# Two heads of attention at a time, new estimates in the planner, two kinds of adds moved from GpSimd to VectorE, and a mixer table stored whole

## The chip, the cores and the metric

One core of one Trainium2 chip runs the kernel. The metric is the device time of one execution in microseconds (us). The engines are TensorE (PE; its weight loads are shown apart as PEld), VectorE (DVE), ScalarE (ACT), GpSimd (POOL) and SyncE (SP), which here issues every DMA. They run side by side and wait for one another by semaphores.

## What is computed

A decoder trunk of two layers on 512 positions of 1024 channels. Each layer has four parts: a half-step gated FFN, a token mixing of attention heads beside a state-space mixer (S5), a second half-step FFN, and a gated input embedding (ple).

```python
# per layer i:  h += 0.5*post(ffn1(h)); h += post(mix(h)); h += 0.5*post(ffn2(h)); h += post(ple(h))
def swiglu(x, w_gate, w_up, w_down):
    return (jax.nn.silu(x @ w_gate) * (x @ w_up)) @ w_down
...
q, k, v, u = jnp.split(rms_norm(h, mix_pre_g) @ w_in, [512, 1024, 1536], axis=-1)
q, k = partial_rotary(q, positions), partial_rotary(k, positions)   # 8 heads of 64
# three causal dilated windows (128,1),(512,4),(2048,16), merged by their softmax denominators
attn = dilated_mixture_attention(q, k, v)
# s5_mixer: 32 groups of 16 channels, 64 complex states each
lam_bar = jnp.exp(lam * dt); b_bar = ((lam_bar - 1.0) / lam)[..., None] * b_mat
_, states = lax.associative_scan(combine, (lam_bar, einsum(u, b_bar)), axis=1)
y = jnp.real(einsum(states, c_mat)) + d_skip * u
y = jax.nn.gelu(y); ssm = y * jax.nn.sigmoid(y @ w_glu + b_glu)
mixed = jnp.concatenate([rms_norm(attn, attn_norm_g), rms_norm(ssm, ssm_norm_g)], axis=-1)
h = h + rms_norm(mixed @ w_out, mix_post_g)
```

## The kernel before, in words

Activations lie transposed: 8 tiles of 128 channels by 512 positions. A product with a weight matrix is made in split precision: weight and activation are each parted into a high and a low float32r half, and `mm3` issues three matmuls (high by high, high by low, low by high) into one PSUM bank. The weights come as 392 units of up to 512 KB in the order of use; each is loaded by SP, its high half is written by ACT and its low half by DVE (128x1024, in the groups of the profile). A unit of 24 matmuls of 512 columns is then PE's work. The sections that close a part (`tail`, then `post`) go by two halves of 256 positions: PE works on the second half while DVE normalises the first and hands it to the next part.

No engine's order is written by hand. `Clock` keeps an estimated time for each engine and each word of memory; `Engine` adds an estimated cost for every instruction that is issued (`Engine.cost`, and the line with `ns =` in `mm`); side work runs in generators that yield the estimated time at which they want to go on, and `step` lets those run that are due before it issues the next three matmuls of the main stream. So every engine's order follows from these estimates: they are not executed, but whoever changes one changes the order.

The stretch with which the change has to do is the mixing (`mix`). The main stream is: u and the first q and k (6 units in halves), v (4 units), q and k of the second pair of heads, the GLU of the state-space branch, q and k of the other pairs, `w_out` in two parts. Beside it run three kinds of side work:

- **The mixer** (`mixer`, two lanes of two octets each; an octet is 8 groups). u is written to DRAM (`scratch_u`) and gathered by 8 DMAs (`gather_u`). For each octet SP loads tables (`tb`, `te`, `tc` from `scratch_t`) and the matrix T of the responses, which `ssm_prep` made in the FFN before and stored as 128x128 in `scratch_g`. T is block-triangular: POOL clears it once for each lane, and 8 DMAs of 64 down to 8 KB place shifted pieces of each response (lines 1517 and 1528 to 1532). PE's first product of an octet needs `tb` and the gathered u.
- **Attention** (`attention`, `head`). The three windows are one softmax with a mask of log counts. For each pair of heads t, and each block of 128 queries qi (3 down to 0), each of the two heads is a task of its own, 6 alive at most (`LIVE`). A task makes scores with two matmuls, one with all 128 rows and one with the head's own 64 rows (`q[rows, c], kl[rows, 0:W]`), then mask and minimum (DVE), exponent (ACT), reciprocal and scaling (DVE), qi+1 transposes (`flip`, line 568), a copy (ACT), and qi+1 products with v of 64 output columns (below: value products).
- **Sums of squares** (`sumsq`): ACT squares, POOL adds; and the rotary (`rotary`), whose last add is POOL's.

All DVE, ACT, POOL and SP instructions have line 353, all matmuls line 562, the transposes line 568. A plain float32 matmul leaves two records in the trace, a float32r matmul or a transpose one.

## Time and profile before

| | |
|---|---|
| median of 3 runs | 2147.78 us (2141.76 to 2147.9) |
| the profiled execution | 2144.88 us, its span 2143.1 us |
| PE busy | 2090.1 us, 98% |
| DVE, ACT, POOL busy | 1334.3, 798.4, 156.1 us |
| mixing, first product of the mixer to the output's tail | 443 to 614 us (layer 0), 1501 to 1672 us (layer 1) |

A row of the timeline merges instructions of one kind: its start, its time, and in brackets how long its engine was idle before it and what ended that. As matmuls are pipelined and their ends modelled, the spacing of a stream is read from one start to the next, or from a long row divided by its count.

### The profile page before, as it was taken

Reading aid. Unit: us, or ns where it says so; the run is one execution under the profiler, and the core shown is the slowest. Engines: PE = TensorE matmul, PEld = TensorE weight load, DVE = VectorE, ACT = ScalarE, POOL = GpSimd, SP = SyncE. Lnnn points to the kernel's source line nnn. Section 1 sums busy time; section 2 is a strip of 40 time slices with the busy share of each in tenths; the row PEclk is TensorE's granted clock in tenths of the full one; section 3 lists DMA queues with packets and bytes.
Section 4 is the critical chain, followed back from the end, with each engine's and each line's share of the span. In section 5 each row is a group of like instructions: output and inputs, shape, how many; then the busy total and the mean of one; then the engine's idle time right before and its main releaser. Section 6 shows DMA issues by size and latency. Waiting matters only on the chain.

```text
span 2143.1 us, 30766 instructions
## 1 busy us (share of the span) xinstructions
PE 2090.1 (98%) x11936; PEld 1780.0 (83%) x11936; DVE 1334.3 (62%) x2516; ACT 798.4 (37%) x1406; POOL 156.1 (7%) x167
## 2 busy tenths in 40 slices
PE   8999999989999999999999999998999999999997
PEld 7888888967789888889998888898777898888897
DVE  5887745776768975446674444467666864444474
ACT  4422333435554322223543222234356533222242
POOL 0000000101120000001200000011011200000022
PEclk9999999999999999999999999999999999999999
DMA  4424434471133534324324233246511333323131
GB/s 157 129 82 152 137 104 138 133 171 40 60 109 113 166 121 125 111 63 154 102 82 148 72 102 114 62 165 141 138 50 50 131 116 110 117 61 127 59 131 67
DMA packets 118145, 236.29 MB, mean 110 GB/s; under 512 B 27120, under 2 KB 58480, under 8 KB 118000
## 3 DMA queue, kind: packets, MB, share of 16 engines
q1 hardware_dynamic: 118000, 234.34, 35.3%
q8 instruction: 93, 1.52, 0.3%
q14 instruction: 52, 0.43, 0.1%
HBM read 208.60 MB, written 25.69 MB: 109 GB/s over the span
## 4 chain that ended last, share of the span: by engine, by line
PE 89%; DVE 6%; DMA 1%; issue 1%; ACT 1%; POOL 1%; SPq 0%; POOLq 0%; ACTq 0%; DVEq 0%
PE ps_all L562 88%; DVE sb_all L353 4%; DVE sr_all L353 2%; PE ps_all L568 1%; DMA sb_all<-scratch_t 1%; ACT sb_all L353 1%; POOL sb_all L353 1%; SPq L353 0%; ACT sr_all L353 0%; DVE z L353 0%; DMA sb_all<-weights 0%; DMA sb_all<-scratch_g 0%; DMA scratch_u<-sb_all 0%; ACT z L353 0%; POOLq L353 0%
## 5 line engine op out<-in xcount | busy, mean ns | idle before, releaser
L562 PE MATMUL ps_all<-sr_all 128*128 128x512 f32 (+2 forms) x7118 | 1447.2, 358 | 16.1 <-ACT sr_all L353 8.6
L562 PEld LDWEIGHTS ps_all<-sr_all 128*128 128x128 f32 (+1 forms) x7118 | 1185.1, 191 | 222.6 <-issue 19.2
L353 ACT ACTIVATE sr_all<-sb_all 128x512 fp32r<-128x512 f32 (+5 forms) x567 | 410.5, 742 | 562.7 <-DVE sb_all L353 398.9
L562 PE MATMUL ps_all<-sr_all,z 128*128 128x512 f32 (+1 forms) x2898 | 572.3, 348 | 0.9 <-DVE sr_all L353 0.9
L353 DVE TENSOR_TENSOR sr_all<-sb_all,sr_all 128x1024 fp32r<-128x1024 f32 (+5 forms) x455 | 417.8, 927 | 184.8 <-ACT sr_all L353 182.5
L562 PEld LDWEIGHTS ps_all<-sr_all,z 128*128 128x128 f32 x2898 | 469.8, 190 | 67.9 <-issue 1.8
L353 DVE TENSOR_TENSOR sb_all<-ps_all,sb_all 128x512 f32<-128x512 f32 (+1 forms) x396 | 244.4, 622 | 367.4 <-PE ps_all L562 361.7
L353 ACT ACTIVATE sb_all<-sb_all 128x256 f32<-128x256 f32 (+3 forms) x390 | 188.6, 490 | 483.2 <-DVE sb_all L353 481.1
L353 POOL TENSOR_TENSOR sb_all<-sb_all 128x256 f32<-128x256 f32 (+3 forms) x159 | 152.3, 960 | 1982.1 <-ACT sb_all L353 1739.1
L353 DVE TENSOR_TENSOR sb_all<-sb_all 128x256 f32<-128x256 f32 (+7 forms) x597 | 233.7, 407 | 22.6 <-DMA scratch_t<-sb_all 7.9
L353 ACT ACTIVATE sb_all<-ps_all 128x512 f32<-128x512 f32 (+5 forms) x228 | 102.9, 466 | 204.5 <-PE ps_all L562 166.8
L353 DVE SCALAR_TENSOR_TENSOR sb_all<-sb_all 128x512 f32<-128x512 f32 (+4 forms) x194 | 115.8, 599 | 65.0 <-ACT sb_all L353 63.3
L353 DVE TENSOR_TENSOR z<-sb_all,z 128x1024 fp32r<-128x1024 f32 (+2 forms) x112 | 120.2, 1075 | 55.3 <-ACT z L353 55.2
L562 PE MATMUL ps_all<-sb_all 128*64 128x128 f32 (+6 forms) x1412 | 127.4, 268 | 27.2 <-DMA sb_all<-scratch_t 12.6
L562 PEld LDWEIGHTS ps_all<-sb_all 128*64 128x64 f32 (+3 forms) x1412 | 108.1, 156 | 53.2 <-issue 27.1
L353 ACT ACTIVATE z<-sb_all 128x1024 fp32r<-128x1024 f32 (+2 forms) x112 | 103.5, 926 | 58.7 <-PE ps_all L562 39.2
L353 DVE TENSOR_SCALAR sb_all<-sb_all 128x32 f32<-128x32 f32 (+7 forms) x147 | 44.1, 306 | 37.3 <-POOL sb_all L353 20.7
L353 DVE SCALAR_TENSOR_TENSOR sb_all<-sb_all,ps_all 128x256 f32<-128x256 f32 x132 | 63.1, 480 | 4.3 <-PE ps_all L562 4.2
L353 DVE SCALAR_TENSOR_TENSOR sr_all<-sb_all,sr_all 128x256 fp32r<-128x256 f32 x96 | 51.8, 549 | 0.2 <-ACT sr_all L353 0.2
L353 DVE CUSTOM_DVE_ANT_0 sb_all<-ps_all,sb_all 128x512 f32<-128x512 f32 (+3 forms) x62 | 28.4, 485 | 34.5 <-PE ps_all L562 30.6
L568 PE MATMUL ps_all<-sb_all 128*128 128x128 f32 x218 | 33.9, 274 | 0.0
L568 PEld LDWEIGHTS ps_all<-sb_all 128*128 128x128 f32 x218 | 26.4, 140 | 7.3 <-issue 1.4
(38 smaller groups left out, 170.3 us busy)
## 6 DMA issues: line engine op xcount, KB each, us to landing
sb_all<-weights SPq DMA_DIRECT2D x263, 512.0 KB, 3.7
sb_all<-weights SPq DMA_DIRECT2D x96, 320.0 KB, 2.9
scratch_t<-sb_all SPq DMA_DIRECT2D x40, 256.0 KB, 3.2
scratch_h<-sb_all SPq DMA_DIRECT2D x80, 128.0 KB, 1.7
sb_all<-scratch_h SPq DMA_DIRECT2D x40, 256.0 KB, 5.8
sb_all<-scratch_t SPq DMA_DIRECT2D x16, 512.0 KB, 6.3
sb_all<-weights SPq DMA_DIRECT2D x32, 192.0 KB, 2.3
sb_all<-xt SPq DMA_DIRECT2D x16, 128.0 KB, 3.7
```

What stands on the lines that cost most here:

```text
L353: return f(*a, **k)
L562: self.nc.tensor.matmul(out, lhsT, rhs, start=start, stop=stop)
L568: self.nc.tensor.transpose(out, x, self.ident)
```

## The change

The planner's estimates are other numbers: latency behind PE 200 ns in place of 170; a float32r matmul at least 110 ns; 100 ns where a matmul's weights change between more and at most 64 rows or columns; a DMA at least 450 ns, and by the length of its runs, with 4000 ns to landing in place of 2000 where these are 512 bytes or less; more for DVE instructions with a per-partition scalar and for the shuffle. `sumsq` and `rotary` add on DVE. `ssm_prep` keeps each response behind 112 cleared columns and stores 8 shifted copies into `scratch_r`, 128x1024 for each octet, and `mixer` loads T from there with one DMA of 512 KB and clears nothing. Attention takes the two heads of a pair in one task (`block`, 3 alive): for qi 0 and 1 both share a PSUM bank and a copy; the second score matmul has all 128 rows, for which `parts` keeps a low half of k for each head in both halves of the partitions (6 slots of the float32r store in place of 5, and two ACT copies of 64x512 more for each pair of heads); and the value products of the two heads alternate.

```diff
-LIVE = 6
+LIVE = 3
-    LAT = 170.0
+    LAT = np.array([200.0, 170.0, 170.0, 170.0, 170.0])
+    SHAPE = 100.0
...
-            self.ck.take(self.name, self.cost(op, outs, ins, k), outs, ins, 2000.0 if op == "dma_start" else 0.0)
+            done = 0.0
+            if op == "dma_start":
+                done = 2000.0 if self.run(*outs, *ins) > 512 else 4000.0
+            self.ck.take(self.name, self.cost(op, outs, ins, k), outs, ins, done)
...
-            return n * outs[0].shape[0] * 4 / 330.0
+            b = n * outs[0].shape[0] * 4
+            return max(450.0, b / 330.0, b / self.run(*outs, *ins) * 2.4)
...
-            return 65 + 0.52 * n
-        return 70 + {"reciprocal": 8.3, "tensor_tensor_scan": 2.08}.get(op, 1.04) * n
+            return 65 + 0.52 * n + 60 * sum(n > words(x) == 1 for x in ins)
+        own = sum(n > words(x) == 1 for x in ins) * 60 + 165 * (op == "stream_shuffle")
+        return 70 + own + {"reciprocal": 8.3, "tensor_tensor_scan": 2.08}.get(op, 1.04) * n
...
-        ns = max(n, lhsT.shape[1]) / 0.6 / share + 4 if lhsT.dtype == F32 else n / 2.4 + 2.5
+        ns = max(n, lhsT.shape[1]) / 0.6 / share + 4 if lhsT.dtype == F32 else max(n / 2.4 + 13.3, 110.0)
+        shape = lhsT.shape[0] > 64, lhsT.shape[1] > 64
+        if shape != self.ck.shape:
+            self.ck.shape = shape
+            ns += self.ck.SHAPE
...
-            self.tt(acc, acc, v, ALU.add, eng=self.po)      # sumsq
+            self.tt(acc, acc, v, ALU.add)
-        self.tt(dst, dst, self.b(b), ALU.add, eng=self.po)  # rotary
+        self.tt(dst, dst, self.b(b), ALU.add)
...
-        gv = self.b(ws)[:, 4 * NW:4 * NW + P]
+        gz = self.b(ws)[:, 4 * NW:4 * NW + (2 * L - 1) * GC]
+        gv = gz[:, (L - 1) * GC:]
+        self.po.memset(gz[:, 0:(L - 1) * GC], 0.0)
...
-            self.sy.dma_start(self.scratch_g[i, o], gv)
...
-            yield self.ck.after(3000.0)
+            for j in range(L):
+                yield self.ck.after(1500.0)
+                self.sy.dma_start(
+                    self.scratch_r[i, o, j * GC:(j + 1) * GC].rearrange("h (g c) -> g h c", g=2 * Q),
+                    gz[:, j * GC:j * GC + P])
...
-        self.po.memset(T, 0.0)
...
-            src = self.scratch_g[i, o].rearrange("(g h) c -> h g c", h=GC)
-            for ti in range(L):
-                j = L - 1 - ti
-                self.sy.dma_start(Tv[j * GC:(j + 1) * GC, :, ti * GC:], src[:, :, 0:(L - ti) * GC])
+            self.sy.dma_start(T, self.scratch_r[i, o])
...
-    def head(self, M, t, hh, qi, bank):
+    def block(self, M, t, qi, bank):
...
-        self.mm(self.pb(bk, W), q[:, c], k[:, 0:W], True, False)
-        self.mm(self.pb(bk, W), q[rows, c], kl[rows, 0:W], False, True)
+        for (q, k, kl), s in zip(parts, sc):
+            self.mm(s, q[:, c], k[:, 0:W], True, False)
+            self.mm(s, q[:, c], kl[:, 0:W], False, True)
...
+        if one:
+            self.act(self.b(bufs[1], 2 * W), self.pb(bks[0], 2 * W))
...
-        for j in range(n):
-            self.mm(self.ps[rows, bank * SEQ + qi * P:bank * SEQ + (qi + 1) * P],
-                    self.b(v[j])[:, t * P + hh * HD:t * P + (hh + 1) * HD], self.b(pt)[:, j * P:(j + 1) * P],
-                    j == 0, j == n - 1)
+        for j in range(n):
+            for hh in range(2):
+                rows = slice(hh * HD, (hh + 1) * HD)
+                self.mm(self.ps[rows, bank * SEQ + qi * P:bank * SEQ + (qi + 1) * P],
+                        self.b(v[j])[:, t * P + hh * HD:t * P + (hh + 1) * HD], pt[hh][:, j * P:(j + 1) * P],
+                        j == 0, j == n - 1, 2)
...
-        got = yield from self.rs.tgets(1, 1, 1, 1, 1)
+        got = yield from self.rs.tgets(1, 1, 1, 1, 1, 1)
...
+        for _, _, l, own, other in heads:
+            self.act(l[other], l[own].bitcast(F32))
```

Every engine's order is new. In the rows below one row is a run of like instructions; PE's float32 matmul is one instruction here.

PE, layer 0, from the last 128x128 that spreads the norm (all of u waits for it) to the first products of the mixer (64x64), before:

```order
L562 MATMUL ps_all<-sb_all 128x1 x2
L562 MATMUL ps_all<-sb_all 128x128 x2
L562 MATMUL ps_all<-sr_all 128x256 x57
L562 MATMUL ps_all<-sr_all,z_75 128x256 x24
L562 MATMUL ps_all<-sr_all 128x256 x24
L562 MATMUL ps_all<-sr_all 128x512 x27
L562 MATMUL ps_all<-sb_all 64x64 x16
L562 MATMUL ps_all<-sr_all 128x512 x18
```

and after:

```order
L583 MATMUL ps_all<-sb_all 128x1 x2
L583 MATMUL ps_all<-sb_all 128x128 x2
L583 MATMUL ps_all<-sr_all,z_75 128x256 x6
L583 MATMUL ps_all<-sr_all 128x256 x96
L583 MATMUL ps_all<-sr_all 128x512 x57
L583 MATMUL ps_all<-sb_all 64x64 x16
L583 MATMUL ps_all<-sr_all 128x512 x18
L583 MATMUL ps_all<-sb_all 64x64 x16
```

The mixer's first product stands behind 57 matmuls of 512 columns and 102 of 256 in place of 27 and 105; in layer 1 behind 54 in place of 30. These are v's.

PE, layer 0, the end of the last pair's attention (128x384, x256 and x128 from `sr_all` alone are scores, 64x128 value products, rows of the other line transposes, the rest `w_out`), before:

```order
L562 MATMUL ps_all<-sr_all,z_4015 128x512 x3
L568 MATMUL ps_all<-sb_all 128x128 x4
L562 MATMUL ps_all<-sb_all 64x128
L562 MATMUL ps_all<-sr_all 128x256 x2
L568 MATMUL ps_all<-sb_all 128x128 x6
L562 MATMUL ps_all<-sr_all,z_4015 128x512 x3
L562 MATMUL ps_all<-sb_all 64x128 x4
L562 MATMUL ps_all<-sr_all 128x256 x2
L562 MATMUL ps_all<-sb_all 64x128 x4
L562 MATMUL ps_all<-sr_all,z_4015 128x512 x3
L562 MATMUL ps_all<-sb_all 64x128 x6
L562 MATMUL ps_all<-sr_all 128x128 x2
```

and after:

```order
L593 MATMUL ps_all<-sb_all 128x128 x8
L583 MATMUL ps_all<-sb_all 64x128 x2
L583 MATMUL ps_all<-sr_all,z_4023 128x512 x3
L593 MATMUL ps_all<-sb_all 128x128 x6
L583 MATMUL ps_all<-sr_all 128x256 x4
L583 MATMUL ps_all<-sr_all,z_4023 128x512 x3
L583 MATMUL ps_all<-sb_all 64x128 x14
L583 MATMUL ps_all<-sr_all,z_4023 128x512 x3
L583 MATMUL ps_all<-sr_all 128x128 x4
L583 MATMUL ps_all<-sr_all,z_4023 128x512 x9
L593 MATMUL ps_all<-sb_all 128x128 x4
L583 MATMUL ps_all<-sr_all,z_4023 128x512 x3
```

Two heads' scores and value products stand together where each head's stood apart. In the whole program the 160 value products, 224 transposes and 128 score matmuls are as many as before; the 64 score matmuls of 64 rows have 128.

SP, layer 0, from the gathering of u on, before:

```order
L353 DMA sb_all<-scratch_u 16x32x64 x8
L353 DMA sb_all<-scratch_t 128x1024
L353 DMA sb_all<-scratch_t 128x512
L353 DMA sb_all<-scratch_t 128x1024
L353 DMA sb_all<-scratch_g 16x8x128
L353 DMA sb_all<-scratch_g 16x8x112
L353 DMA sb_all<-scratch_g 16x8x96
L353 DMA sb_all<-scratch_g 16x8x80
L353 DMA sb_all<-scratch_g 16x8x64
L353 DMA sb_all<-scratch_g 16x8x48
L353 DMA sb_all<-scratch_g 16x8x32
L353 DMA sb_all<-scratch_g 16x8x16
```

and after:

```order
L358 DMA sb_all<-scratch_u 16x32x64 x8
L358 DMA sb_all<-scratch_t 128x1024
L358 DMA sb_all<-scratch_t 128x512
L358 DMA sb_all<-scratch_t 128x1024
L358 DMA sb_all<-scratch_r 128x1024
L358 DMA sb_all<-scratch_t 128x1024
L358 DMA z_3388<-scratch_t 128x512
L358 DMA sb_all<-scratch_t 128x1024
L358 DMA sb_all<-scratch_r 128x1024
L358 DMA sb_all<-weights 128x1024 x4
```

Eight loads of T have become one, and the second lane's tables follow four issues behind the first lane's in place of eleven. In the FFN before, 8 stores to `scratch_g` have become 64 to `scratch_r` (2 to 3 in a row between weights). On POOL 124 of 159 adds and powers are gone, 96 of them 128x256 and 28 128x512; DVE has them.

## Rows read from the trace of the kernel before

**Rows 1.** The page, busy us of an engine, share of the span, instructions.

```profile
PE 2090.1 (98%) x11936; PEld 1780.0 (83%) x11936; DVE 1334.3 (62%) x2516; ACT 798.4 (37%) x1406; POOL 156.1 (7%) x167
```

**Rows 2.** The page, shares of the chain that ended last.

```profile
PE 89%; DVE 6%; DMA 1%; issue 1%; ACT 1%; POOL 1%; SPq 0%; POOLq 0%; ACTq 0%; DVEq 0%
```

**Rows 3.** Busy time by stretch: us, PE, PEld, DVE, ACT, POOL busy (instructions), clock, DMA.

```profile
653.00:1011.00 358.00, 358.00 (x1831) 302.94 (x1830) 226.44 (x391) 114.63 (x173) 8.29 (x10) 1.00 0.39 124
1011.00:1021.00 10.00, 9.06 (x67) 8.25 (x65) 9.83 (x21) 4.41 (x11) 3.90 (x5) 1.00 0.01 2
443.20:613.80 170.60, 166.67 (x1136) 124.38 (x1136) 117.25 (x279) 85.75 (x180) 18.71 (x13) 0.97 0.29 83
1501.40:1671.60 170.20, 165.48 (x1132) 125.65 (x1132) 114.80 (x279) 85.33 (x180) 19.21 (x13) 0.96 0.28 78
613.80:652.60 38.80, 36.38 (x286) 35.72 (x286) 33.70 (x72) 18.36 (x44) 12.71 (x16) 0.96 0.39 140
```

**Rows 4.** PE in order of time, layer 0's attention: start, us, instructions.

```profile
465.22 1.09 PE L562 MATMUL ps_all<-sb_all 128*64 128x128 f32 x16
...
499.21 0.70 PE L562 MATMUL ps_all<-sr_all 128*128 128x256 f32 x2
499.84 0.87 PE L562 MATMUL ps_all<-z,sb_all 128*64 128x128 f32 x6
...
514.13 10.48 PE L562 MATMUL ps_all<-sr_all 128*128 128x512 f32 x45
...
580.52 1.09 PE L562 MATMUL ps_all<-sb_all 128*64 128x128 f32 x8
...
583.41 0.58 PE L562 MATMUL ps_all<-sr_all 128*128 128x128 f32 x2
583.92 0.65 PE L562 MATMUL ps_all<-sb_all 128*64 128x128 f32 x4
...
620.18 7.72 PE L562 MATMUL ps_all<-sr_all 128*128 128x256 f32 x63
```

**Rows 5.** PE in order of time, where it waits in either layer's mixing.

```profile
443.23 1.97 PE L562 MATMUL ps_all<-sb_all 128*64 128x64 f32 x32 [5.50 <-DMA sb_all<-scratch_t]
...
643.24 1.05 PE L562 MATMUL ps_all<-sb_all 128*128 128x1 f32 x8 [1.66 <-POOL sb_all L353]
...
1501.36 1.98 PE L562 MATMUL ps_all<-sb_all 128*64 128x64 f32 x32 [7.10 <-DMA sb_all<-scratch_t]
```

**Rows 6.** Groups by line and shape: busy us, mean ns, idle before.

```profile
L353 DVE TENSOR_TENSOR sb_all<-sb_all 128x256 f32<-128x256 f32 x273 | 120.0, 441 | 7.8 <-ACT sb_all L353 0.5
...
L353 POOL TENSOR_TENSOR sb_all<-sb_all 128x256 f32<-128x256 f32 x99 | 83.2, 843 | 1458.4 <-ACT sb_all L353 1450.0 <-DVE sb_all L353 3.4 <-issue 3.1
...
L353 POOL TENSOR_TENSOR sb_all<-sb_all 128x512 f32<-128x512 f32 x28 | 43.6, 1561 | 337.8 <-DVE sb_all L353 210.6 <-ACT sb_all L353 118.7 <-issue 5.4
L353 DVE TENSOR_TENSOR sb_all<-sb_all 128x512 f32<-128x512 f32 x65 | 43.1, 688 | 8.4 <-DMA scratch_t<-sb_all 5.7 <-DMA scratch_u<-sb_all 1.8
...
L353 ACT ACTIVATE sr_all<-sb_all 64x512 fp32r<-64x512 f32 x48 | 30.1, 627 | 16.2 <-POOL sb_all L353 15.6
```

**Rows 7.** SP's queue in order of time, layer 0: start, us, issues.

```profile
434.75 2.42 SPq L353 DMA_DIRECT2D sb_all<-scratch_t  x3
437.29 8.51 SPq L353 DMA_DIRECT2D sb_all<-scratch_g  x8
```

**Rows 8.** POOL and DVE in order of time, a stretch of squares' sums.

```profile
621.85 5.22 POOL L353 TENSOR_TENSOR sb_all<-sb_all 128x256 f32<-128x256 f32 x6 [4.42 <-ACT sb_all L353]
...
626.60 0.76 DVE L353 TENSOR_TENSOR sb_all<-sb_all 128x256 f32<-128x256 f32 x1
...
628.04 0.42 DVE L353 TENSOR_TENSOR sb_all<-sb_all 128x256 f32<-128x256 f32 x1
```

More of the change, by code (lines that the diff above doesn't have):

```diff
@@ L243, in peek @@
             m, s = self._span(ap)
-            t = max(t, (m[0][s] + np.where(m[1][s] != c, self.LAT, own)).max())
+            t = max(t, (m[0][s] + np.where(m[1][s] != c, self.LAT[m[1][s]], own)).max())
         for ap in outs:
@@ L1619, in rotary @@
         self.stt(self.b(b), self.b(b), scale, self.b(M["sin"]))
-        self.tt(dst, dst, self.b(b), ALU.add, eng=self.po)
+        self.tt(dst, dst, self.b(b), ALU.add)
         self.sl.put(b)
-    def head(self, M, t, hh, qi, bank):
+    def block(self, M, t, qi, bank):
         v = M["v"]
-        q, k, kl = (self.r(b) for b in M["parts"][t][hh])
+        parts = [[self.r(b) for b in x] for x in M["parts"][t]]
         n = qi + 1
         W = n * P
-        rows = slice(hh * HD, (hh + 1) * HD)
-        yield self.ck.ready(q, k, kl[rows])
-        while len(self.sl.free) < 2:
+        one = 2 * W <= SEQ
+        yield self.ck.ready(*[x for p in parts for x in p])
+        need = 2 if one else 4
+        while len(self.sl.free) < need:
@@ L1655, in head @@
-        self.sl.put(p)
-        yield self.ck.ready(self.b(pt, W))
-        for j in range(n):
-            self.mm(self.ps[rows, bank * SEQ + qi * P:bank * SEQ + (qi + 1) * P],
-                    self.b(v[j])[:, t * P + hh * HD:t * P + (hh + 1) * HD], self.b(pt)[:, j * P:(j + 1) * P],
-                    j == 0, j == n - 1)
-        self.sl.put(pt)
+        bufs = [self.sl.get() for _ in range(need)]
+        p = [self.b(bufs[0])[:, hh * W:(hh + 1) * W] if one else self.b(bufs[hh], W) for hh in range(2)]
@@ new lines, in block @@
+        pt = [self.b(bufs[1])[:, hh * W:(hh + 1) * W] if one else self.b(bufs[2 + hh], W) for hh in range(2)]
+        c = slice(qi * P, (qi + 1) * P)
+        bks = []
+        sc = []
+        for hh in range(2):
+            if not (one and hh):
+                bks.append((yield from self.tbank()))
+            sc.append(self.pb(bks[-1], W, W * hh if one else 0))
+        for (q, k, kl), s in zip(parts, sc):
+            self.mm(s, q[:, c], k[:, 0:W], True, False)
+            self.mm(s, q[:, c], kl[:, 0:W], False, True)
@@ new lines, in block @@
+        dens = []
+        for hh in range(2):
+            st = self.o_st + 2 * (self.nst % 32)
+            self.nst += 1
+            m, den = self.w(st, 1), self.w(st + 1, 1)
+            dens.append(den)
+            self.ve.tensor_tensor_reduce(
+                out=p[hh], in0=sc[hh], in1=self.w(self.o_const + C_MASK + SEQ - W, W), scale=-1.0,
+                scalar=3e38, op0=ALU.add, op1=ALU.min, accum_out=m)
+            self.act(p[hh], p[hh], AF.Exp, scale=-1.0, bias=m, accum_out=den)
@@ new lines, in block @@
+        self.free(*bks)
+        for hh in range(2):
+            yield self.ck.ready(p[hh])
+            self.ve.reciprocal(dens[hh], dens[hh])
+            self.ts(p[hh], p[hh], dens[hh])
+        yield self.ck.ready(*p)
+        bks = []
+        for hh in range(2):
+            if not (one and hh):
+                bks.append((yield from self.tbank()))
+            for j in range(n):
+                self.flip(self.pb(bks[-1], P, (W * hh if one else 0) + j * P), p[hh][:, j * P:(j + 1) * P])
+            if not one:
+                self.act(pt[hh], self.pb(bks[-1], W))
@@ L1673, in parts @@
             self.act(a[own], q[own])
-        yield max(self.ck.written(a[own]) for a, _, own, _ in heads)
-        for a, _, own, other in heads:
+        yield max(self.ck.written(a[own]) for a, _, _, own, _ in heads)
+        for a, _, _, own, other in heads:
             self.tt(a[other], q[own], a[own].bitcast(F32), ALU.subtract)
         yield self.ck.written(k)
-        for _, b, own, _ in heads:
+        for _, b, _, own, _ in heads:
             self.act(b[own], k[own])
-        yield max(self.ck.written(b[own]) for _, b, own, _ in heads)
@@ L1681, in parts @@
-        for _, b, own, other in heads:
-            self.tt(kl[own], k[own], b[own].bitcast(F32), ALU.subtract)
+        yield max(self.ck.written(b[own]) for _, b, _, own, _ in heads)
+        for _, b, l, own, other in heads:
+            self.tt(l[own], k[own], b[own].bitcast(F32), ALU.subtract)
             self.act(b[other], k[own])
+        yield max(self.ck.written(l[own]) for _, _, l, own, _ in heads)
+        for _, _, l, own, other in heads:
+            self.act(l[other], l[own].bitcast(F32))
@@ L1684, in parts @@
         self.sl.put(M["q"][t], M["k"][t])
         M["rs"][t] = got
-        M["parts"][t] = [(got[2 * hh], got[2 * hh + 1], got[4]) for hh in range(2)]
+        M["parts"][t] = [tuple(got[3 * hh:3 * hh + 3]) for hh in range(2)]
     def attention(self, i, M):
@@ L1697, in attention @@
             for qi in range(3, -1, -1):
-                for hh in range(2):
-                    while sum(not d[0] for d in live) >= LIVE:
-                        yield self.ck.after(100.0)
-                    d = self.ck.spawn(self.head(M, t, hh, qi, bank))
-                    live.append(d)
-                    mine.append(d)
-                    live = [d for d in live if not d[0]]
+                while sum(not d[0] for d in live) >= LIVE:
+                    yield self.ck.after(100.0)
+                d = self.ck.spawn(self.block(M, t, qi, bank))
+                live.append(d)
+                mine.append(d)
+                live = [d for d in live if not d[0]]
             ends.append(self.ck.spawn(self.attended(i, t, M, bank, mine)))
```

50 lines of the change are left out of this document (24 added, 26 removed).

## The prediction, as it was made

> **What bounds the kernel now.** The page's busy shares come first: PE 2090.1 of 2143.1 us [rows 1]; then the chain, 89% PE and 6% DVE [rows 2]. So PE's stream sets the time, and the question is what it holds besides useful columns, and where it stands still. Busy time by stretch says where [rows 3]: in an FFN (653 to 1011) PE has no gap at all, so nothing can be won there by another order. The mixing is different. From the mixer's first product to the tail of `w_out` it takes 170.6 us in layer 0 and 170.2 in layer 1, PE nearly full, DVE busy 117.25 and 114.80 (69 and 67%). Between parts DVE is the full one: 9.83 of 10 us from 1011 on, 33.70 of 38.80 at the end of layer 0's mixing. Last I read PE in order of time inside the mixing, for the price of single products, and its waits.
>
> **Scores.** A long run of 45 matmuls of 512 columns takes 0.233 us each, one of 63 with 256 columns 0.1225 [rows 4]; the line through both gives 0.067 for 128. A head's score pair of 256 columns should thus take 0.245 and takes 0.63 from its start to the next row's (499.21 to 499.84); one of 128 should take 0.13 and takes 0.51 (583.41 to 583.92). The excess is 0.385 and 0.38. The pair holds the one matmul with 64 rows, and the array goes over to it and back. After, all scores have 128 rows and the change of shape is gone. 64 pairs at 0.38: 24.3 us off PE's stream. If the excess were half a cost of small batches that stays, 12; more than 24.3 isn't to be seen.
>
> **Value products.** Four of one head take 1.09 us and two 0.65, so one takes 0.22; eight of the mixer's products of the very same shape (128 rows, 64 columns, 128 moving), whose halves of the columns alternate, take the same 1.09 [rows 4]. Alternating, a product costs half. 160 of them save 160 x 0.11 = 17.6; some stood by chance next to the other head's already, and I take 15. Bounds: 0, were they not to overlap, and 17.6 with up to 2 us more for the fewer groups.
>
> **The wait for the first table.** PE stands 5.50 us at 443.23 and 7.10 at 1501.36 until the table behind the gathered u has landed [rows 5]. The new order puts 30 and 24 matmuls of 512 columns (v) before that product, 30 x 0.233 = 7.0 and 24 x 0.233 = 5.6 us. The gather itself starts where it did, behind the same norm. So the first wait goes and 1.5 of the second stays: 11 us. These matmuls are missing later as filler, but PE still has q and k of the second pair (45 matmuls on end at 514 [rows 4]) when the lanes are done, so I charge nothing; were the filler missed, all 11 come back.
>
> **What DVE gets.** 96 adds of 128x256 at 0.441 and 28 of 128x512 at 0.688 (POOL's took 0.843 and 1.561) are 61.6 us of new DVE work [rows 6]. In the FFNs it lies beside PE, with DVE at 226.44 of 358. At the seams DVE is full, and there an add on it delays the next part's first operands. The two seams mixing to FFN are solid DVE work for 20 us: six adds of the second half, 6 x 0.44 = 2.6 each, 5.3 together. The others have PE work in stock (ple's up-projection, the first half's products of u). Against it, PE waited for POOL's slow last add, 1.66 us at 643.24 [rows 5] and so at some other seams, partly ended now. Net +2 (bounds -6.6, four such waits given back and the adds covered, and +21, the adds paid at eight seams).
>
> In the mixing the stretch loses 19.6 us of PE work (half of 24.3 + 15) and 7.0 or 5.6 that went ahead, 144.0 and 145.0 remain. DVE has there some 12 of the 128x512 adds more, 8.2: 125.5 and 123.0, which is 87 and 85%. That is much for a queue in order, on which weight splits, two mixer lanes and masks stand between one another; I charge 2 us a layer, 4 (bounds 0 and 25: the rival below). ACT's 16 copies of 64x512, 0.627 each [rows 6], are 10 us on an engine that is half idle (85.75 of 170.6); they delay each pair's first score by under 1 us, while other pairs run.
>
> **T and its stores.** SP needed 8.51 us for the eight loads of one octet [rows 7]; one load takes about 0.4. But PE's first wait is for what stands before T in the queue, and the next lane's table, 8 us earlier, meets a PE that has v to do: 0 (bounds -3 and +1, as 512 KB replace 288). The 56 further stores, 64 KB each, in FFNs: DMA is busy there at 0.39 [rows 3], and if they hold up a weight load it is by their issue of about 0.4 us; the units are loaded three ahead. 0 (up to +3).
>
> **One rule against the change.** [Rows 8]: while POOL works through six adds without a break to 627.07, a DVE add of 128x256 that starts at 626.60 takes 0.76 us, the next, alone, 0.42. The Trainium skill, SBUF — State Buffer, "SBUF: two separate sides", says that VectorE and GpSimd share one pair of ports under an exclusive lock and that an instruction on the one shuts the other out as a whole. By that rule the moved adds are cheaper than their durations: if each of the 124 had held up DVE by 0.34, DVE would get 42 of its 61.6 us back, and the seams' +2 would be about -1. The trace agrees where DVE has work just then; elsewhere it isn't shown, and the sum goes by the durations.
>
> **Sum.** -24.3 - 15 - 11 + 2 + 4 = -44.3 us. Against the profiled execution's 2144.9 that is 2100.6; the median of the runs lies 2.9 above it, within their spread, so I say 2101.
>
> **Rivals.** (1) *DVE limits the mixing.* Its 125.5 us need a share that no whole stretch of the mixing has yet had; for it speaks the 69%, against it the seams, where it runs at 98%. If 79% is its best, the stretches take 159 and 156: 1.5 us (v in front of the first product, where only 5.50 were idle) - 11.6 - 14.2 + 2 = -22.3, 2123. The Trainium skill, TensorEngine Tiling (Array Packing), "PSUM Bottleneck", warns of just this: tiling speeds up TensorE, not the evacuation of PSUM. (2) *DVE paces it as it stands*, its gaps being the latency of chains and not want of work: then its share stays 69 and 67%, the stretches take 183 and 182, 12.4 and 11.8 more than before, and with 1.5 + 2 the kernel takes 2173, slower. It decides from a share below some 74% (248.5 us of DVE in the 337 of both stretches that would leave the sum at nothing). Against it: PE idles only 3.9 and 4.7 us there [rows 3], so DVE's gaps are times when PE was the late one. (3) *Alternating value products don't overlap in attention*, because each pair waits for its own copies: 2116. The copies of both heads are done before the first product, which speaks against it. (4) *The waits shrink too*, as the estimates now know more of what PE waits for: the idle 3.9 and 4.7 go, and the 2 and 4 charged to DVE don't come, 14.6 less: 2086. (5) *The change doesn't do what it says* in the table load: worth 0 in any case.
>
> **Chances.** Forecast 0.58, own range 2092 to 2111; (4) 0.17; (1) 0.17; (3) 0.05; (2) 0.03. The range leaves out the slow rival and the ends of (1) and (4): 2083 to 2125. About 0.3%, 6.4 us, can be told from no change here. Faster: all but (2) and the outer part of (1), 0.94; within, 0.03; slower, 0.03.
>
> **What would show it.** No matmul with 64 rows by 128 columns is left, and two score pairs of 256 columns follow each other at about 0.12 a matmul; sixteen records of value products take about 1.09. At the mixer's first product the wait is gone in layer 0 and under 2.5 in layer 1. The stretch from there to the tail is 143 to 149 us long, DVE at 85% or more, and PE's idle time in it below 10 us. At the seam out of the mixing DVE's solid work is up to 2.6 us longer. It would be wrong if PE's waits for DVE in the mixing rose above 15 us a layer, if the wait for the table came back elsewhere (for T, or as idle time before the GLU), or if attention started so late that its last pair ended behind `w_out`'s first part.

## The result, and the profile after

The changed kernel takes 2160.35 us (median of 7 runs, 2154.46 to 2165.54) against 2147.78: ratio 1.0066, 95% interval 1.0051 to 1.0081. Forecast were 2101 us, 2083 to 2125. It is slower by 0.7%, and the profile shows that TensorE's work shrank all the same.

The page's busy times and its chain, to be held against [rows 1, 2], and the span with the mean granted clock, before (first row of the second block) and after:

```profile
PE 2062.0 (96%) x11936; PEld 1773.6 (82%) x11936; DVE 1357.6 (63%) x2640; ACT 803.2 (37%) x1406; POOL 27.5 (1%) x41
...
PE 76%; DVE 15%; ACT 4%; issue 3%; DMA 2%; SPq 1%; POOL 0%; ACTq 0%; DVEq 0%; POOLq 0%
```

```profile
core 0: 2143.1 us, clock 0.988
core 0: 2154.3 us, clock 0.979
```

PE is busy 28 us less, and idle 2154.3 - 2062.0 = 92.3 us where it was 53.0. DVE's part of the chain went from 6 to 15%. With two levels, 2.4 and 1.2 GHz, a mean clock of 0.979 means that 2 x 0.021 x 2154 = 90 us ran at the lower one; before, at 0.988, it was 51. An estimate from this: the 39 us more at half the clock cost at most 20 us of PE's busy time, so its products themselves became 28 to 48 us cheaper.

Where it went, by stage, from the first product of one part to that of the next (us of the profiled executions; two numbers are the two layers; the four columns on the right are runs told of below):

| stage | before | after | u_adds | late | u_T | late_T_slack |
|---|---|---|---|---|---|---|
| FFN 1 of layer 0, seventh projection to closing | 311.7 | 316.4 | 315.0 | 315.0 | 315.0 | 311.7 |
| into the mixing, up to v | 41.7, 40.4 | 45.2, 47.0 | 42.4, 42.4 | 39.6, 39.6 | 47.1, 45.2 | 39.6, 39.6 |
| v to `w_out`'s tail | 179.9, 181.9 | 167.9, 165.7 | 166.6, 166.2 | 167.3, 169.7 | 162.5, 166.1 | 161.5, 163.5 |
| out of the mixing | 27.5, 27.6 | 35.0, 33.1 | 27.5, 27.6 | 28.9, 30.7 | 35.6, 33.4 | 30.7, 27.2 |
| FFN 2, first six projections | 42.5, 42.5 | 47.0, 46.8 | 40.5, 40.5 | 47.4, 42.1 | 43.0, 43.4 | 39.5, 39.5 |
| FFN 2 of layer 0, the rest | 311.8 | 316.0 | 314.9 | 315.9 | 313.8 | 311.7 |

The mixings gained 28.2 us. The six stretches around them lost 31.9, the two FFNs beside which the next table is prepared 8.9; the other stages gained 1.4. That is the 11.2 us between the two profiled executions.

The mixing as the forecast had cut it, from the first mixer product on (columns as in [rows 3]):

```profile
452.20:609.60 157.40, 138.85 (x1105) 111.09 (x1104) 116.73 (x289) 87.71 (x178) 1.05 (x1) 0.95 0.27 95
1518.10:1673.30 155.20, 140.68 (x1110) 112.26 (x1110) 118.39 (x291) 86.78 (x177) 1.01 (x1) 0.95 0.27 95
```

PE is idle 18.6 and 14.5 us there, against 3.9 and 4.7, and DVE's share is 74 and 76%, not 87 and 85.

The closing of a part and the FFN behind it, in the changed kernel, and the same work in u_adds, where POOL makes the adds:

```profile
607.10:642.20 35.10, 29.50 (x231) 28.98 (x229) 24.41 (x55) 12.77 (x28) 2.14 (x2) 0.94 0.35 124
642.20:689.20 47.00, 41.52 (x310) 40.62 (x311) 40.55 (x102) 21.53 (x45) 2.28 (x4) 0.90 0.39 124
```

```profile
601.50:629.00 27.50, 27.48 (x222) 27.17 (x221) 22.26 (x42) 12.81 (x28) 10.92 (x12) 0.97 0.52 187
629.00:669.50 40.50, 38.78 (x319) 37.91 (x318) 33.95 (x73) 19.89 (x44) 4.86 (x7) 1.00 0.36 116
```

In the first stretch of the changed kernel DVE is busy 24.4 of 35.1 us: it isn't full. Its timeline shows what it does (for one column tile: the product in PSUM times a scale, the add of that to the tile, the add of the square; in brackets the idle time and what ended it):

```profile
618.06 0.43 DVE L358 TENSOR_TENSOR sb_all<-sb_all 128x256 f32<-128x256 f32 x1 [0.48 <-ACT sb_all L358]
618.40 0.42 DVE L358 TENSOR_TENSOR sb_all<-ps_all,sb_all 128x256 f32<-128x256 f32 x1
618.85 0.42 DVE L358 TENSOR_TENSOR sb_all<-sb_all 128x256 f32<-128x256 f32 x1
619.76 0.42 DVE L358 TENSOR_TENSOR sb_all<-sb_all 128x256 f32<-128x256 f32 x1 [0.48 <-ACT sb_all L358]
```

The row at 618.85 writes the tile, ACT squares it, and the row at 619.76 adds the square. DVE's queue is in order, so the next tile's work stands behind this round trip: 1.70 us a tile. In u_adds a tile takes 0.80:

```profile
610.20 0.42 DVE L358 TENSOR_TENSOR sb_all<-ps_all,sb_all 128x256 f32<-128x256 f32 x1
610.65 0.43 DVE L358 TENSOR_TENSOR sb_all<-sb_all 128x256 f32<-128x256 f32 x1
611.00 0.42 DVE L358 TENSOR_TENSOR sb_all<-ps_all,sb_all 128x256 f32<-128x256 f32 x1
```

All such waits of DVE together, by form (busy and mean; idle time ahead, and what ended it):

```profile
L358 DVE TENSOR_TENSOR sb_all<-sb_all 128x256 f32<-128x256 f32 x369 | 155.9, 425 | 55.1 <-ACT sb_all L358 47.6 <-DMA sb_all<-bc 0.5
```

The same form before the change stood 7.8 us [rows 6]. And PE, at the end of the stretch, waits for the last tile's sum (second row); in the FFN beside which the mixer's tables are prepared it waits for one of them (first row):

```profile
157.26 1.10 PE L583 MATMUL ps_all<-sb_all 128*32 128x128 f32 x14 [2.86 <-DVE sb_all L358]
...
639.95 0.38 PE L583 MATMUL ps_all<-sb_all 128*128 128x1 f32 x2 [3.32 <-DVE sb_all L358]
```

### The profile page after: what moved, and what is told of

It is laid out like the page before. It is cut to its first block, busy times and chain, and to the rows that moved or that the text cites. A ratio compares the mean times of both kernels' runs of the same rounds, so it can differ in the third digit from the quotient of the medians.

```text
span 2154.3 us, 30549 instructions
## 1 busy us (share of the span) xinstructions
PE 2062.0 (96%) x11936; PEld 1773.6 (82%) x11936; DVE 1357.6 (63%) x2640; ACT 803.2 (37%) x1406; POOL 27.5 (1%) x41
## 4 chain that ended last, share of the span: by engine, by line
PE 76%; DVE 15%; ACT 4%; issue 3%; DMA 2%; SPq 1%; POOL 0%; ACTq 0%; DVEq 0%; POOLq 0%
PE ps_all L583 75%; DVE sb_all L358 11%; DVE sr_all L358 3%; ACT sb_all L358 2%; ACT sr_all L358 1%; DVE z L358 1%; PE ps_all L593 1%; DMA sb_all<-scratch_t 1%; SPq L358 1%; DMA sb_all<-weights 1%; ACT z L358 0%; DMA sb_all<-pt 0%; POOL sb_all L358 0%; DMA scratch_u<-sb_all 0%; ACT L358 0%
## 5 line engine op out<-in xcount | busy, mean ns | idle before, releaser
L583 PE MATMUL ps_all<-sr_all 128*128 128x512 f32 (+1 forms) x7154 | 1429.0, 356 | 37.1 <-ACT sr_all L358 23.1
L583 PEld LDWEIGHTS ps_all<-sr_all 128*128 128x128 f32 x7154 | 1187.8, 192 | 225.4 <-ACT sr_all L358 24.9
L358 ACT ACTIVATE sr_all<-sb_all 128x1024 fp32r<-128x1024 f32 (+5 forms) x568 | 410.6, 742 | 601.8 <-DVE sb_all L358 466.4
L358 DVE TENSOR_TENSOR sr_all<-sb_all,sr_all 128x1024 fp32r<-128x1024 f32 (+5 forms) x456 | 406.7, 901 | 214.6 <-ACT sr_all L358 213.2
L358 DVE TENSOR_TENSOR sb_all<-sb_all 128x256 f32<-128x256 f32 (+7 forms) x720 | 288.0, 414 | 74.4 <-ACT sb_all L358 58.6
L583 PE MATMUL ps_all<-sb_all 128*64 128x128 f32 (+6 forms) x1388 | 111.5, 266 | 26.5 <-DVE sb_all L358 14.5
L583 PEld LDWEIGHTS ps_all<-sb_all 128*64 128x64 f32 (+3 forms) x1388 | 95.4, 154 | 46.7 <-DVE sb_all L358 17.7
L358 DVE TENSOR_SCALAR sb_all<-sb_all 128x32 f32<-128x32 f32 (+8 forms) x144 | 39.3, 281 | 31.4 <-POOL sb_all L358 18.6
L358 POOL TENSOR_TENSOR sb_all<-sb_all 128x2 f32<-128x2 f32 (+2 forms) x35 | 27.0, 771 | 2122.0 <-DVE sb_all L358 1425.9
L358 DVE SCALAR_TENSOR_TENSOR sr_all<-sb_all,sr_all 128x256 fp32r<-128x256 f32 x96 | 45.0, 478 | 0.4 <-ACT sr_all L358 0.4
L593 PEld LDWEIGHTS ps_all<-sb_all 128*128 128x128 f32 x213 | 26.2, 143 | 16.1 <-DVE sb_all L358 10.5
```

Source lines behind the costliest of these rows:

```text
L358: return f(*a, **k)
L583: self.nc.tensor.matmul(out, lhsT, rhs, start=start, stop=stop)
L593: self.nc.tensor.transpose(out, x, self.ident)
```

## The experiments

Each is timed against the kernel before and told as a ratio with its 95% interval; 0.01 of it is 21.5 us. A difference between two runs is the difference of their ratios.

**u_adds**, the adds back on POOL.

```diff
-            self.tt(acc, acc, v, ALU.add)
+            self.tt(acc, acc, v, ALU.add, eng=self.po)
...
-        self.tt(dst, dst, self.b(b), ALU.add)
+        self.tt(dst, dst, self.b(b), ALU.add, eng=self.po)
```

> The changed kernel with the 124 adds of the sums of squares and the rotation back on POOL. In the changed kernel the six stretches before and behind the mixings (from the mixing's first projection to v, from w_out's tail to the FFN, the FFN's first up and gate products) are 31.9 us longer than before. Theory 1, crowding: DVE is the last to finish there and each add on it delays PE, the clock then falls as well; with the adds back on POOL at least 20 of the 31.9 us go and the kernel takes 0.990 to 0.997 of before. Theory 2, the plan: the estimates order PE's products too close behind DVE's and ACT's work, whoever adds; the stretches stay 20 us or more longer, ratio 1.002 to 1.010.

Measured 0.9891 (0.9859 to 0.9922), 37.6 us off the changed kernel. The six stretches are 33.2 us shorter, the mixings as they were (table). Theory 1 holds in kind: the adds were it. Whether their load or their place in the queue, the run called late tells.

**u_est**, the estimates of before (those of DVE, of DMA and of a matmul as well).

```diff
-    LAT = np.array([200.0, 170.0, 170.0, 170.0, 170.0])
-    SHAPE = 100.0
+    LAT = np.array([170.0] * 5)
+    SHAPE = 0.0
...
-                done = 2000.0 if self.run(*outs, *ins) > 512 else 4000.0
+                done = 2000.0
```

> The changed kernel with the estimates of before (latencies, change of shape, matmul, DMA, DVE). Theory 1, crowding: only the two waits in the FFNs behind the mixer's tables (2.9 and 2.3 us, with 5.5 and 5.2 us of delay) go, the stretches around the mixings stay long: ratio 1.000 to 1.006. Theory 2, the plan: these stretches come back to their lengths of before too, some 30 us in all, and the attention's gain shows: ratio 0.982 to 0.992.

1.0109 (1.0090 to 1.0128): both theories miss. The two FFNs are back at 311.8 us each, but the mixings take 175.2 and 176.6. The new estimates earn about 18 us in the mixings and lose about 9 in the FFNs. Of the 18, 11 are the wait for the table, which is back with the old estimates, though T comes in one load:

```profile
449.26 1.98 PE L581 MATMUL ps_all<-sb_all 128*64 128x64 f32 x32 [5.12 <-DMA sb_all<-scratch_t]
...
1520.49 1.98 PE L581 MATMUL ps_all<-sb_all 128*64 128x64 f32 x32 [6.53 <-DMA sb_all<-scratch_t]
```

**u_att**, the attention of before: `head` for `block`, `parts` and `attention` of before.

```diff
-LIVE = 3
+LIVE = 6
...
-                d = self.ck.spawn(self.block(M, t, qi, bank))
+                    d = self.ck.spawn(self.head(M, t, hh, qi, bank))
```

> The changed kernel with the attention of before (one head a task, 64-row second score product, six tasks alive). If the pairs of heads gave what their matmuls show (39 us less on TensorE by the forecast) and the waits come from elsewhere, the kernel loses it: ratio 1.018 to 1.028. If the pairs themselves brought the new waits in the mixing (PE idle 17.4 and 14.9 us, against 8.5 and 11.0 with 5.5 and 7.1 of them for the table), the gain was theirs to lose and the ratio stays 1.002 to 1.012.

1.0183 (1.0164 to 1.0201): the pairs of heads are worth 25 us even here; the mixings become 179.2 and 187.8 us. PE's busy time, at the same granted clock, is 39.5 us longer (2062.0 in the changed kernel):

```profile
PE 2101.5 (96%) x11936; PEld 1786.5 (82%) x11936; DVE 1360.8 (62%) x2640; ACT 796.8 (36%) x1406; POOL 27.3 (1%) x41
...
core 0: 2188.0 us, clock 0.979
```

**u_T**, T as before, its stores, loads and clear, and the plan's numbers with them.

```diff
...
-            self.sy.dma_start(T, self.scratch_r[i, o])
+            src = self.scratch_g[i, o].rearrange("(g h) c -> h g c", h=GC)
+            for ti in range(L):
+                j = L - 1 - ti
+                self.sy.dma_start(Tv[j * GC:(j + 1) * GC, :, ti * GC:], src[:, :, 0:(L - ti) * GC])
```

> The changed kernel with T written and loaded as before (8 stores of 64 KB, eight loads an octet, POOL's clear). If the layout of T costs nothing, as forecast, the ratio stays within 1.004 to 1.009. If the paced stores delay the preparation or the weight loads in the FFNs, the FFN stretches of 316 us come back to 312 each and the ratio falls by 0.003 to 0.005; if the single load is what removed the wait for the table, PE waits 5 us or more there again, ratio 1.010 or more.

0.9971 (0.9961 to 0.9982): 20 us off the changed kernel, though no PE wait for T shows in the changed kernel. The gain lies in several stages (table), so the next runs part the transfers from the plan.

**t_phys**, the old transfers under the new plan; `only_planned` books a transfer in the plan and issues none.

```diff
...
-            self.sy.dma_start(T, self.scratch_r[i, o])
+            src = self.scratch_g[i, o].rearrange("(g h) c -> h g c", h=GC)
+            for ti in range(L):
+                j = L - 1 - ti
+                self.nc.sync.dma_start(Tv[j * GC:(j + 1) * GC, :, ti * GC:], src[:, :, 0:(L - ti) * GC])
+            self.only_planned(T, self.scratch_r[i, o])
```

> The changed kernel with its own plan to the last estimate, so with the same order on TensorE, VectorE and ScalarE, but T really stored and loaded as before (8 stores, eight loads an octet, POOL's clear). Going back to the old T took 0.9% off the changed kernel in the run before. If the new layout costs that by its transfers, the same comes back here: ratio 0.995 to 0.999. If it cost it by the order that the plan makes of other numbers, nothing comes back: 1.003 to 1.009, or more where a product now waits for T's eight loads (5 us a layer, 1.009 to 1.012).

1.0081 (1.0061 to 1.0101): nothing comes back. So the new transfers are not what costs, as forecast. The old ones under this plan make PE wait for tables again, 4.2 us in layer 0's mixing (first row) and 2.1 in layer 1's, where the changed kernel has 0.5 in all:

```profile
PE ps_all L583 <- DMA sb_all<-scratch_t: 4.2, 2, 2.6
...
PE ps_all L583 <- DMA sb_all<-scratch_t: 2.1, 1, 2.1
```

**plan_T**, the reverse: the new transfers, and the plan reckons with eight loads and POOL's clear.

```diff
...
-            self.sy.dma_start(T, self.scratch_r[i, o])
+            self.nc.sync.dma_start(T, self.scratch_r[i, o])
+            src = self.scratch_g[i, o].rearrange("(g h) c -> h g c", h=GC)
+            for ti in range(L):
+                j = L - 1 - ti
+                self.only_planned(Tv[j * GC:(j + 1) * GC, :, ti * GC:], src[:, :, 0:(L - ti) * GC])
```

> The changed kernel with its new T (64 stores, one load an octet), but the plan reckons with the eight small loads and POOL's clear of before; the order changes, the transfers do not. If the plan's belief that T is there early is what costs, this takes the 20 us off that the old T did: ratio 0.994 to 1.000. If the preparation's stores are behind it, it stays at 1.003 to 1.009.

0.9980 (0.9969 to 0.9991), 18.5 us off the changed kernel: the plan's numbers for T are it. By stage, of the 11.3 us between the two profiled executions 5.6 lie in the mixings (164.3 and 163.7 us) and 6.5 in FFN 2's first six projections (43.7 and 43.6). PE's waits in layer 0's mixing, changed kernel and plan_T (waited for: us, times, longest):

```profile
PE ps_all L593 <- DVE sb_all L358: 5.4, 3, 3.0
PE ps_all L583 <- ACT z L358: 4.5, 1, 4.5
PE ps_all L583 <- ACT sb_all L358: 4.3, 2, 2.5
PE ps_all L583 <- ACT sr_all L358: 3.0, 2, 1.9
...
```

```profile
PE ps_all L583 <- ACT sr_all L358: 4.0, 2, 2.2
PE ps_all L583 <- DVE z L358: 3.7, 1, 3.7
PE ps_all L593 <- DVE sb_all L358: 3.4, 2, 2.7
PE ps_all L583 <- ACT sb_all L358: 0.4, 1, 0.4
...
```

17.4 us of waits become 12.0. Why an earlier T in the plan makes later waits for ACT, and a longer stretch behind the mixing, was not followed to its end.

**pace**, the eight stores one behind the other, then 3 us of pause.

```diff
             for j in range(L):
-                yield self.ck.after(1500.0)
...
+            yield self.ck.after(3000.0)
```

> The changed kernel with the eight stores of an octet's T issued one behind the other and the 3 us pause of before after them, not 1.5 us before each. If the stores' pacing is behind the 20 us, 10 us or more go: ratio 0.995 to 1.002. If not, the time stays (1.003 to 1.009), or rises where eight stores at once hold up a weight load.

1.0069 (1.0050 to 1.0088): the pacing isn't it.

**lat190** and **lat210**, one latency of the plan 5% down or up.

```diff
-    LAT = np.array([200.0, 170.0, 170.0, 170.0, 170.0])
+    LAT = np.array([190.0, 170.0, 170.0, 170.0, 170.0])
```

> The changed kernel with one number of the plan 5% smaller: 190 ns from TensorE to another engine in place of 200. No instruction costs more or less. If the order settles the time only by its rules, this stays at 1.0066 within 0.002. If the accident of the order weighs as much as the 20 us that going back to T's old layout brought, it moves by 0.004 or more, either way.

> The changed kernel with 210 ns for the same latency: a second draw of the order. Within 0.002 of 1.0066 if such numbers do not matter by themselves; further off, either way, if they do.

1.0046 (1.0031 to 1.0061) and 1.0061 (1.0046 to 1.0076). These two changes of a number move the time by 4 and 1 us; T's 20 are more than that. Two draws are few, so it is not shown how far a change of order alone can move the time.

**late**, all adds on DVE, each add of a square one tile later in the queue.

```diff
...
             self.act(v, x, AF.Square)
+            if late:
+                self.tt(acc, acc, self.b(late[0], x.shape[1]), ALU.add)
+                self.sl.put(late.pop())
...
+            if late is not None:
+                late.append(t)
+                return
             self.tt(acc, acc, v, ALU.add)
```

> The changed kernel, all adds on DVE, but each add of a square in the closing of a part comes one column tile later in DVE's queue, behind the next tile's adds. In the changed kernel DVE stands 0.48 us before such an add, until ACT has squared what DVE has just written (47.6 us in all before its 369 adds of 128x256). Theory 1a, the queue in order: this round trip to ACT is what the adds cost, the waits go, and the stretches around the mixings lose most of what they had gained: ratio 0.988 to 0.996. Theory 1b, the load: 0.44 us of DVE work an add is what they cost; the load is the same, and the ratio stays 1.001 to 1.008.

0.9894 (0.9877 to 0.9912): the same as with POOL, with DVE's work unchanged. The same rows in it, and the row by form:

```profile
609.64 0.76 DVE L358 TENSOR_TENSOR sb_all<-sb_all 128x256 f32<-128x256 f32 x2
610.32 0.42 DVE L358 TENSOR_TENSOR sb_all<-ps_all,sb_all 128x256 f32<-128x256 f32 x1
610.77 0.76 DVE L358 TENSOR_TENSOR sb_all<-sb_all 128x256 f32<-128x256 f32 x2
```

```profile
L358 DVE TENSOR_TENSOR sb_all<-sb_all 128x256 f32<-128x256 f32 x369 | 153.1, 423 | 7.6 <-DMA sb_all<-bc 0.5
```

A tile takes 1.13 us, and of 55.1 us of idle time 7.6 are left. Theory 1a holds: the round trip was the price, not the load. In the profiled execution the six stretches are 25.8 us shorter than in the changed kernel; FFN 2's first part in layer 0 stays at 47.4 (table). Like u_adds, the run has an order of its own, so a part of its gain may be the order's; that both give 37 us, and that the idle time in front of the adds goes, speaks for the round trip.

**adds_T**, adds on POOL and the old T; **adds_T_slack**, with the response products of the preparation ordered 4 us later:

```diff
-            yield self.ck.ready(cv[0], cv[1])
+            yield self.ck.ready(cv[0], cv[1]) + 4000.0
```

> The changed kernel with the adds back on POOL and T as before; the estimates and the attention stay. If the two effects are apart from one another (37 us and 20 us off the changed kernel's 2160), they add up to 2104, ratio 0.977 to 0.983. If what T brought was an accident of the order (other products, other waits of DVE), nothing is left of it beside the adds: 0.986 to 0.992.

> As the run before it, and the mixer's response products in the FFNs are ordered 4 us later than the plan thinks their operands ready. In the changed kernel TensorE waits 2.9 and 2.3 us there and the two FFN stretches are 316.4 and 316.0 us long against 311.7 and 311.8; the wait should go, the stretches come back to 312, and the kernel take 5 to 9 us less than the run before it (0.2 to 0.4%). If the stretches are long for the stores' issue and not for this wait, nothing changes.

0.9840 (0.9826 to 0.9855) and 0.9819 (0.9804 to 0.9834). The two effects add up to 48.5 us, not to 58. With the 4 us the wait in the FFNs goes (back to 311.7 and 311.8 us); the time falls by 4.5 us, at the edge of what the intervals can tell.

**score64** and **serial**, on adds_T_slack with its plan kept: the second score product on 64 rows; the value products of one head behind the other's.

```diff
-            self.mm(s, q[:, c], kl[:, 0:W], False, True)
+            self.mm(s, q[:, c], kl[:, 0:W], False, True, rows=slice(0, HD))
```

```diff
-        for j in range(n):
-            for hh in range(2):
+        for hh in range(2):
+            for j in range(n):
```

> The run before (adds on POOL, T as before, response products 4 us later; ratio 0.9819) with the same plan and order, but the second score product has 64 rows again; it leaves out the correction from the upper 64 rows. The forecast's first term, 64 pairs at 0.38 us for the change of shape, makes this 24.3 us slower: ratio 0.990 to 0.995. If the pairs' excess was not the change of shape, or hides behind waits for VectorE and ScalarE, it is under half of that: 0.980 to 0.987.

> The run with ratio 0.9819 with the value products of one head behind those of the other, not in turns. The forecast's second term, 160 x 0.11 us, makes it 15 to 18 us slower: ratio 0.987 to 0.992. If the two heads' products do not overlap, or TensorE would wait in any case, the ratio stays 0.980 to 0.984.

0.9933 (0.9913 to 0.9953), which is 24.5 us slower, where 24.3 were forecast; and 0.9833 (0.9818 to 0.9847), 3 us slower where 15 to 18 were, which the intervals don't tell from nothing (0.9804 to 0.9834 for adds_T_slack); PE is busy 3.7 us longer (2053.3 against 2049.6). A group of sixteen records (eight products, two heads) at the same place of both, in turns in adds_T_slack (first) and not in serial:

```profile
521.36 1.09 PE L583 MATMUL ps_all<-sb_all 128*64 128x128 f32 x16
```

```profile
523.80 1.58 PE L583 MATMUL ps_all<-sb_all 128*64 128x128 f32 x16
```

**rot**, on adds_T_slack with the rotation's adds on DVE (the second edit of u_adds left out), and **late_T_slack**, the edits of late, u_T and the 4 us together.

> The run with ratio 0.9819 (squares' and rotation's adds on POOL, old T, response products 4 us later) with the 16 adds of the rotation, 128x512, on DVE. The rotation's add waits for no other engine: its product stands on DVE just before it. If only the round trip to ScalarE makes an add dear, this gives nothing back or a little, as POOL's 1.3 us adds leave the way to q and k: 0.977 to 0.984. If DVE's load is dear in the mixing, it is slower: 0.985 to 0.990.

> All adds on DVE, those of the squares one tile late, with the old T and the response products 4 us later. The late adds gave 0.9894 and the adds on POOL 0.9891, each with the changed kernel's T; if they are worth the same here too, the ratio is 0.979 to 0.985; if POOL as a third engine matters once the other waits are gone, 0.985 to 0.990.

0.9840 (0.9822 to 0.9858) and 0.9778 (0.9763 to 0.9792). With the rotation's adds on DVE the kernel is 4.5 us slower than adds_T_slack, with intervals that overlap: no difference that can be told. The second run, at 2098.8 us (2097.2 to 2100.2), beats the kernel before by 48 us and the changed one by 62; its clock:

```profile
core 0: 2095.4 us, clock 0.989
```

**mended**, every part of the change, with the edits of late, plan_T and the 4 us.

> The changed kernel with all its parts (adds on DVE, 64 stores and one load of T, pairs of heads, estimates), but the squares' adds one tile late, the plan reckoning with T's eight loads, and the response products 4 us later. If these three are what the forecast missed, the ratio is 0.976 to 0.984, as with the old T (0.9778). If the new T's transfers cost something after all, 0.984 to 0.992.

0.9827 (0.9810 to 0.9843), 2111.8 us. The three causes are worth 51 us of the changed kernel's 2160. Against late_T_slack 10.5 us remain; in the profiled executions the two mixings are 13 us longer (166 and 172), with another order there. Whether the order or the transfers cost them is open, though t_phys speaks against the transfers.

## Why the prediction was wrong

**The step that failed** is the one on DVE's adds: "Net +2 (bounds -6.6, four such waits given back and the adds covered, and +21, the adds paid at eight seams)". It priced an add at its own duration, 0.44 us. What it measured is 37.6 us (u_adds) or 36.9 (late), because each add of a square waits 0.48 us for ACT, with the next tile's work queued behind it. On POOL that wait stood in POOL's queue, and PE waited for POOL no more than 9.5 us in the whole kernel before (us, times, longest):

```profile
PE ps_all L562 <- POOL sb_all L353: 9.5, 10, 1.7
```

The forecast did not ask what is queued behind the new wait, since the change reads as a move of work and not as a new wait. The Trainium skill, PSUM — Partial Sum Buffer, "Engine vs sequencer instructions", calls the queues of ScalarE, VectorE and GpSimd strictly first in, first out; the trace agrees, 0.48 us a tile, and late shows what it is worth.

**Where the miss lies, in the forecast's terms.** The profiled execution took 2156.25 us where the sum said 2100.6. The six stretches around the mixings grew by 31.9 us where all seams had +2; the mixings from the mixer's first product on took 157.4 and 155.2 us where 146 and 147 were forecast (2 us of crowding each included), 19.6 us more; the FFNs grew by 8.9 where nothing stood.

**Scores, -24.3:** right; 24.5 measured with all else kept (score64).

**Value products, -15:** the mechanism is right (the records overlap), its size isn't. Taking turns saves 0.49 us on the eight products of two heads at the place shown, 3 us in all by time. A group of four took 1.09 us [rows 4], but eight in one group, not in turns, take 1.58 and not twice 1.09: part of what the forecast ascribed to the turns comes from having one group where there were two. What in a group's start costs that wasn't tried. Both terms together came out on PE's busy time, 39.5 us (u_att) of 39.3 forecast; with 25.3 for the scores' shape (2074.9 against 2049.6 in score64) and 3.7 for the turns, some 10 are left for the fewer groups, an estimate, as the runs have different orders. In time the whole attention was worth 25 us in the changed kernel by the ratios. Between the two profiled executions it is 33.7, and PE idles 5.8 us more in the changed kernel.

**The table, -11:** right at the mixer's first product. In layer 0 no wait is left, in layer 1 it is 0.45 us:

```profile
1518.14 1.06 PE L583 MATMUL ps_all<-sb_all 128*64 128x64 f32 x29 [0.45 <-DMA sb_all<-scratch_t]
```

But idle time before the GLU came behind it, which the forecast had named as a sign of being wrong: in layer 0 PE stands 11.7 us between the mixer's first product and the next long run of projections at 517.69, where it stood 2.8 before. Missing filler is not the main cause. In u_est 30 of v's matmuls stand ahead of that product (27 before, 57 in the changed kernel), PE waits for the table, and still stands 8.3 us in the same stretch; in plan_T 57 stand ahead and PE stands 5.8.

**Crowding in the mixing, +4, and rival 1:** the stretches came out at rival 1's lengths (157.4 and 155.2 against 159 and 156), but not for its reason. DVE's share is 74 to 76%, and u_adds, without the adds on DVE, leaves the mixings as long. PE waits there in single places behind chains of ACT and DVE: in layer 0, 11.8 us of its 17.4 are waits for ACT and 5.6 for DVE, so the sign of over 15 us of waits for DVE did not come. That is nearer to rival 2's reason, the latency of chains, at rival 1's length. Other numbers in the plan (plan_T) move these waits.

**T, 0:** right for the transfers (t_phys), wrong for the kernel: the estimate of T's load is part of the planner's input, and its change cost 18 to 20 us. The order that the other estimates make was in the sum only as the table's wait. They gave 18 us in the mixings (u_est against the changed kernel), 11 of them that wait, and took 9 in the FFNs, where PE now waits 2.86 us for a response product's operand.

**The clock** was missing from the sum. The granted clock fell in stretches in which PE had waited just before: 0.90 in FFN 2's first part with 5.5 us of waits, 1.00 for the same products in u_adds with 1.7. Of the 6.5 us between the two, 3.8 are waits; the other 2.7 are within what the lower clock can cost (0.90 of 47 us means 9.4 us at the lower level, an estimate of up to 4.7 us).

**The weighed rule** on the ports came true for DVE's busy time: it grew by 23.3 us, though 124 adds of 0.43 and 0.69 us, 60 us, were added; 37 were given back, and 42 had been the estimate. Against u_adds, from which the changed kernel differs by these adds and by the order, it grew by 26.5, from 1331.1 us:

```profile
PE 2043.7 (96%) x11936; PEld 1759.6 (83%) x11936; DVE 1331.1 (63%) x2516; ACT 804.4 (38%) x1406; POOL 157.9 (7%) x165
```

It did not help, as DVE's load was not what PE waited for.

What was to show the steps: the 64-row scores are gone, and sixteen value records take 1.18 us, 1.11 to the next row's start; score pairs of 256 columns take 0.14 a matmul (597.82 to 598.38, the way in included) where 0.12 was forecast:

```profile
585.33 1.18 PE L583 MATMUL ps_all<-sb_all 128*64 128x128 f32 x16
586.44 0.97 PE L583 MATMUL ps_all<-sr_all 128*128 128x512 f32 x3
...
597.82 0.72 PE L583 MATMUL ps_all<-sr_all 128*128 128x256 f32 x4
598.38 0.86 PE L583 MATMUL ps_all<-sr_all,z 128*128 128x512 f32 x3
```

The mixing's length, DVE's share and PE's idle time all failed their marks. So did the seam out of the mixing: the stretch is 7.5 and 5.5 us longer where 2.6 us of DVE's work were allowed, and DVE's work in it isn't solid.

## What to carry to other kernels

When an operation moves to another engine, ask first whose result it waits for: on an in-order queue an add behind a round trip to another engine costs the trip for all that stands behind it, and one place later in the queue the wait is nearly gone. Where a planner sets the order, another number for one transfer is a change of the whole order and has to be timed alone, with the transfers held and the plan changed, and the other way round. Price a wait of TensorE at more than its length, since the lower granted clock behind it came on top here (39 us more at the lower level beside 39 us more of idle time).

## What the runs showed of the hardware

POOL's adds slow DVE's instructions beside them: in u_adds a multiply-and-subtract of 128x256 takes 0.96 us while a POOL add runs, which starts 0.12 us before it (the first two rows); in the changed kernel, with POOL idle, the same form takes 0.48 (the third):

```profile
624.16 0.96 DVE L358 SCALAR_TENSOR_TENSOR sr_all<-sb_all,sr_all 128x256 fp32r<-128x256 f32 x1
```

```profile
624.04 0.79 POOL L358 TENSOR_TENSOR sb_all<-sb_all 128x256 f32<-128x256 f32 x1 [1.76 <-ACT sb_all L358]
```

```profile
641.46 0.48 DVE L358 SCALAR_TENSOR_TENSOR sr_all<-sb_all,sr_all 128x256 fp32r<-128x256 f32 x1
```

As forecast, one matmul of 64 rows among those of 128 costs 0.38 us a pair by the rows before, and all of it shows in the time, 24.5 us over 64 pairs (score64).
